# Values and gates of two HGRN2 units projected together at 512 columns, with the units of a block in another order

## The chip, the cores and the metric

The kernel runs on one core of one Trainium2 chip. The metric is device time in microseconds (us); the figure for a kernel is the median of its runs. One further execution is recorded by the hardware profiler; its time and its span (first to last instruction) stand beside the median below. The engines are named as in the profile: PE is TensorE's matmul, PEld its weight load, DVE VectorE, ACT ScalarE, POOL GpSimd, SP the engine that issues nearly all DMAs here.

## What is computed

One layer of a decoder trunk over 2048 tokens of width 1024, in float32, conditioned on a vector `c`. Cut to what matters here:

```
mod = silu(c) @ w_ada + b_ada                  # 6 x 1024
sh1, sc1, g1, sh2, sc2, g2 = split(mod, 6)
h = rms_norm(x) * (1 + sc1) + sh1
proj = h @ w_in                                # split into the three groups of heads
#   retention (4 heads), HGRN2 (8 heads: q, f, value i, gate g), GLA (4 heads)
o_h = rms_norm(gated_state(silu(q), key(f), i, log_f)) * silu(g)      # HGRN2; the others alike
x = x + g1 * (concat(o_r, o_h, o_a) * head_gain) @ w_out
h = rms_norm(x) * (1 + sc2) + sh2
u = causal_conv3(h @ w_up) + conv_b
x = x + g2 * (silu(u_gate) * u_val) @ w_down
out = rms_norm(x) * final_gain
```

The gated state is a causal recurrence with a decay for each key channel, made in chunks.

## The kernel before

**Tiling.** The sequence is cut into four blocks (`b` = 0 to 3) of 512 tokens. A matmul product of float32 precision is made of three matmuls (`split3`, L230): each operand is held as a high part (rounded to the matmul's type) and a low part (the rest), and high x high, high x low and low x high are summed in PSUM. Weights come in pieces of 128 x 1024 numbers (512 KB). `piece` (L212) loads a raw piece, ACT rounds it to the high part, and the low part is made by DVE the first time and kept in DRAM (`kept`), from which later blocks load it. There are three buffers for high parts, three for low parts and two for raw pieces.

**Units.** Seven units work on each block, in the order of `ORDER` (L35): four HGRN2 units `h` of two heads (`unit_h`, L680), one GLA unit `g` of four heads in two halves (`unit_g`, L717) and two retention units `r` (`unit_r`, L761). An h unit projects `f` and `q` with the channels on partitions (`cf_gemm`, 512 tokens as columns, tiles `pshfh` and `pshqh`), and its value and gate with the tokens on partitions (`tf_gemm`, L254, 256 columns: 128 of value, 128 of gate, tile `psvgh`). In `tf_gemm` 4 token tiles x 8 slices of the contraction x 3 give 96 matmuls of 256 columns. GLA and retention use `tf512` (L272), which takes two such column groups at a time: 96 matmuls of 512 columns into four PSUM banks. The evacuation makes a copy (value), a sigmoid on ACT and a product on DVE (gate): `tok_evac` (L510) by two token tiles at a time, `tok_evac4` (L519) by one.

**Chains.** After the projections of a unit its recurrence runs as a chain (`gated`, L579; `retention`, L793): seven levels, each of four small matmuls (L603) and some DVE operations, then the state update (`u`, which needs the value tile `v`), the output, its normalisation (`post`) and, later, a transpose (L545). PE's order is written by hand: the class `Clock` counts PE time, and the steps of the chains are put between the projection matmuls at due times. Only one chain runs at a time; the next one starts when it yields `None`.

**Other engines.** DVE, ACT, POOL and SP are ordered when the program is built, by program position; `high_priority(offset)` moves instructions ahead by that much (or back, where it is negative), and an instruction takes its place when its buffers are free by the builder's reckoning. Each engine then issues in that fixed order, SP its DMAs too.

**Work between the units.** `out_half(b, 0)` (L904), the first half of the output projection, runs at the end of block b and starts the residual tiles `x1`, loaded on the tag `xy` (four buffers, each of two tiles). `out_finish(b)` (L926) makes the second half after the first unit of block b + 1, adds the residual (L919), and its `then` (L937) scales the result for the channel mixer and stores it (`h2d`). For block 0 the `x1` tiles are stored to DRAM first, and `then` is put off to the end of block 1, with reloads. The same four `xy` buffers serve the conditioning rows (`ada`, L193: a 512 KB load `wada` and one DVE reduction each; rows still to be made stand in the list `later`, and each weight piece takes one), the sums of channel-mixer weights (`weight_sums`, tiles `wsd`, `wsu`) and the sums of scaled inputs (`early_sums`, tiles `es`). The loop over blocks and units is at L1048.

Of the kernel before, what the change touches and what calls it, by code (L numbers as in the profile page):

```python
# [9 lines left out]
F32 = mybir.dt.float32  # L10
# [21 lines left out]
NSB = 2  # L32
SB = 2 * TB

ORDER = [("h", 0), ("g", 0), ("h", 1), ("h", 2), ("h", 3), ("r", 0), ("r", 1)]  # L35
KTILES = [t for kind, u in ORDER for t in {"h": [2 + u], "g": [6, 7], "r": [u]}[kind]]


# [62 lines left out]
def trunk(ctx, tc, xT, vecs, cvec, cst, rope, msk, wada, win, walow, wgla, wout, wup, wdown, out):  # L101
# [167 lines left out]
                        adv(6 * M256)  # L269
        return pss  # L270

    def tf512(name, i):  # L272

        pss = [acc_ps(f"ps{name}_{c}") for c in range(NCH)]
        for q4 in range(4):
            half, sub = q4 // 2, q4 % 2
            src = win[i + half:i + half + 3:2][:, :, sub * 512:(sub + 1) * 512].rearrange("a p n -> p a n")
            if later:
                ada(later.pop(0))
            with tc.high_priority(offset=50):  # L280
                raw = pw.tile([P, 2, 512], F32, tag="wraw", name=f"r{name}_{q4}", bufs=NRAW)
                nc.sync.dma_start(raw[:], src)
                hi = pw.tile([P, 2, 512], F32R, tag="whi", name=f"h{name}_{q4}")
                lo = pw.tile([P, 2, 512], F32R, tag="wlo", name=f"l{name}_{q4}")
                S.copy(hi[:], raw[:])
                key = f"t{i}_{q4}l"
                flat = lo[:].rearrange("p a n -> p (a n)")
                if key in kept:
                    nc.sync.dma_start(flat.bitcast(F32), kept[key][:])
                else:  # L290
                    with tc.high_priority(offset=HOT):
                        V.tensor_tensor(lo[:], raw[:], hi[:], op=ALU.subtract)
                    keep(key, flat)
            for c in range(NCH):
                cs = slice(c * P, (c + 1) * P)
                for kk in range(2):
                    k = half * 4 + sub * 2 + kk
                    sl = slice(kk * 256, (kk + 1) * 256)
                    split3(pss[c][:].rearrange("p (a n) -> p a n", a=2), (h[k][:, 0, cs], h[k][:, 1, cs]),
                           (hi[:, :, sl], lo[:, :, sl]), k == 0, k == KD - 1)  # L300
                    adv(3 * M512)
        return pss
# [201 lines left out]

    def tok_tiles(name):

        return (pu.tile([P, NCH, P], F32, tag="v", name="v" + name, bufs=3),
                pu.tile([P, NCH, P], F32, tag="sg", name="sg" + name, bufs=3))

    def tok_evac(vsg, pss):  # L510
        v, sg = vsg
# [67 lines left out]
    def gated(name, b, ui, pos, kq, decay, subs, qk, sel):  # L579
# [56 lines left out]
                S.copy(q[r0:r1, 0, :], q[r0:r1, 1, :])  # L636
        adv(4 * MF)
        yield 1.8
        for q, rows, v, sg in subs:
            ps = late_ps("u" + name)  # L640
            for c in range(NCH):
                T.matmul(ps[:, c * P:(c + 1) * P], kT[:, c, :], v[:, c, :], start=True, stop=True)
            with tc.high_priority(offset=CHAIN):
                for c in range(NCH):
                    for hh, (r0, r1) in enumerate(rows):
                        es = slice(64 * hh, 64 * hh + 64)
                        dst = Sst[r0:r1, (b * NCH + c + 1) % NS, es]
                        u = ps[r0:r1, c * P + hh * 64:c * P + hh * 64 + 64]
                        if b == 0 and c == 0:
                            V.tensor_copy(dst, u)  # L650
                        elif c < NCH - 1 or b < NB - 1:
                            V.scalar_tensor_tensor(dst, Sst[r0:r1, (b * NCH + c) % NS, es], cur[r0:r1, c:c + 1], u,
                                                   op0=ALU.mult, op1=ALU.add)
# [23 lines left out]
            adv(4 * MF)  # L677


    def unit_h(b, u, pos):  # L680
        nm = f"h{b}_{u}"
        kq = pu.tile([P, TB], F32, tag="k", name="k" + nm, bufs=3)
        f = pu.tile([P, TB], F32, tag="f", name="f" + nm, bufs=3)
        e = pu.tile([P, TB], F32, tag="e", name="e" + nm)
        ps = cf_gemm("hf" + nm, 4 * u + 1)
        sf, sn = tmp("sf" + nm), tmp("sn" + nm)
        S.activation(sf[:], ps[:], AF.Sigmoid)
        S.activation(sn[:], ps[:], AF.Sigmoid, scale=-1.0)
        V.tensor_scalar(f[:], sf[:], oml[:, u:u + 1], lb[:, u:u + 1], op0=ALU.mult, op1=ALU.add)
        V.tensor_scalar(kq[:], sn[:], oml[:, u:u + 1], None, op0=ALU.mult)  # L690
        ps = cf_gemm("hq" + nm, 4 * u)
        sq = tmp("sq" + nm)
        S.activation(sq[:], ps[:], AF.Sigmoid)
        V.tensor_tensor(sq[:], ps[:], sq[:], op=ALU.mult)
        qk = tmp("qk" + nm)
        V.tensor_tensor(qk[:], sq[:], kq[:], op=ALU.mult)
        rows = [(0, 64), (64, 128)]
        q = new_qbd(nm, rows)
        for hh, (r0, r1) in enumerate(rows):
            V.tensor_tensor(q[r0:r1, hh, :], sq[r0:r1, :], f[r0:r1, :], op=ALU.mult)  # L700
        decay = decays(f, e)
        subs = [(q, rows, *tok_tiles(nm))]
        clock.chain(gated(nm, b, u, pos, kq, decay, subs, qk, selh), 9.0 if b == u == 0 else 6.0)
        tok_evac(subs[0][2:], tf_gemm("vg" + nm, 4 * u + 2))

    alow = p1.tile([P, KD, 32], F32R, tag="alow", name="alow")
    gup = p1.tile([32, P], F32, tag="gup", name="gup")
# [9 lines left out]
    def unit_g(b, pos):  # L717
# [37 lines left out]
        pss = tf512(f"vg{nm}", 18)  # L755
        for i in range(2):
            tok_evac4(subs[i][2:], pss, 256 * i)

    rots = {}

    def unit_r(b, r, pos):  # L761
# [2 lines left out]
            rots[b] = pu.tile([P, NCH, 2, 32], F32, tag="rope", name="rope" + nm, bufs=1)  # L764
            nc.sync.dma_start(rots[b][:], rope[b])
        cos, sin = (rots[b][:, :, i, :] for i in range(2))
        kk = pu.tile([P, NCH, P], F32, tag="kk", name="kk" + nm)
        kc = pu.tile([P, TB], F32, tag="k", name="kc" + nm, bufs=3)
        q = new_qbd(nm, [(0, 64), (64, 128)])
        vsg = tok_tiles(nm)  # L770
# [155 lines left out]
    def out_finish(b, after_pieces=None, begun=None):  # L926
# [8 lines left out]
            nc.sync.dma_start(x1d[b, m][:], rows[m])  # L935

        def then():  # L937
            with tc.high_priority(offset=HOT if b < NB - 1 else -100):
                for m in range(KD):
                    t = rows[m] if b == NB - 1 else tmp(f"t2_{b}_{m}")[:]  # L940
                    if b == 0:
                        nc.sync.dma_start(t, x1d[b, m][:])
                    else:
                        nc.sync.dma_start(x1d[b, m][:], rows[m])
                    V.scalar_tensor_tensor(t, rows[m] if b else t, SC2[:, m:m + 1], bc[:], op0=ALU.mult, op1=ALU.mult)
                    S.activation(t, t, AF.Identity, bias=SH2[:, m:m + 1])
                    nc.sync.dma_start(h2d[b, m][:], t)
            done.add(("n2", b))
# [98 lines left out]
    jobs = [job for k in range(NF // 2) for job in (("d", k), ("u", 2 * k + 1))] + [("u", 0)]  # L1047
    for b in range(NB):  # L1048
        pos = 0
        if b == NB - 1:  # L1050
            later += range(40, 48)
        for i, (kind, u) in enumerate(ORDER):
            if i == len(ORDER) - 3 and b + 1 < NB:
                norm1_stat(b + 1)
# [10 lines left out]
            pos += 2 if kind == "g" else 1  # L1065
            if b == 1 and i == 5:
                assert not later
                clock.until(lambda: put_off)
                put_off.pop()()
            if i == 0 and b:  # L1070
                clock.until(lambda: None not in oTs[b - 1])
                out_finish(b - 1)
            for w in ws:
# [484 lines left out]
```

## Time and profile before

| | |
|---|---|
| median of 3 runs | 2565.36 us (2562.51 to 2572.84) |
| profiled execution | 2567.58 us, span 2565.8 us |
| ACT, POOL busy | 1134.1 us, 160.0 us |
| DMA | 525.13 MB, mean 205 GB/s |
| mixing stage | about the first 1250 us |
| channel mixer | the rest |

In the rows, L232 to L234 are the three matmuls of `split3`, whatever product they belong to, so products are told apart by the tile that they write. A group's line gives busy time and mean duration; durations of matmuls overlap, so starts, not durations, give the rate. In a timeline row stand start, duration, engine, line, operation, output and inputs, and in brackets the idle time before it and what ended that.

### The profile page before, as it was taken

How to read it: one execution, taken by the hardware profiler on the slowest of the kernel's cores; microseconds unless marked ns; L12 is line 12 of the kernel's file. 1: busy time of each engine (PE TensorE's matmuls, PEld its weight loads, DVE VectorE, ACT ScalarE, POOL GpSimd, SP SyncE). 2: the span in 40 equal slices, each digit the busy share in tenths (PEclk: the TensorE clock that was granted, in tenths of full speed). 3: DMA queues.
4: the chain of work that ended last, by engine and by line, in shares of the span. 5: the costliest groups of instructions: out<-in, count | busy, mean ns of one | idle time of the engine just before them, and what ended most of it. 6: DMA issues, size and time to landing. Idle time of an engine off the chain costs nothing.

```text
span 2565.8 us, 36953 instructions
## 1 busy us (share of the span) xinstructions
PE 2485.1 (97%) x13090; PEld 2122.6 (83%) x13090; DVE 1996.1 (78%) x3626; ACT 1134.1 (44%) x1890; POOL 160.0 (6%) x287
## 2 busy tenths in 40 slices
PE   5999999999999998999999999999999999999998
PEld 4898888988889896898778888888878888888887
DVE  8877888767679777686788888887688778778666
ACT  3333334434443334333554545555444554455542
POOL 1000010000000000000010000000001001000000
PEclk9999999999999999999999999999999999999999
DMA  8644468654598747985654445477675454447763
GB/s 307 219 165 132 150 221 312 231 181 160 195 317 295 272 157 233 320 309 186 202 187 162 153 149 163 157 239 257 219 225 186 150 154 145 146 142 245 225 190 132
DMA packets 227721, 525.13 MB, mean 205 GB/s; under 512 B 25264, under 2 KB 28368, under 8 KB 227536
## 3 DMA queue, kind: packets, MB, share of 16 engines
q1 hardware_dynamic: 224336, 512.28, 60.2%
q0 software_dynamic: 3200, 10.49, 1.2%
q8 instruction: 103, 1.69, 0.3%
q14 instruction: 82, 0.67, 0.1%
HBM read 397.37 MB, written 125.30 MB: 204 GB/s over the span
## 4 chain that ended last, share of the span: by engine, by line
PE 87%; DVE 6%; DMA 2%; issue 1%; ACT 1%; POOL 0%; SPq 0%; DVEq 0%; ACTq 0%; POOLq 0%
PE X L232 6%; PE X L234 6%; PE X L233 6%; PE lvh L603 4%; PE Z L233 3%; PE Z L234 3%; PE dX L234 3%; PE Z L232 3%; PE dX L233 3%; PE dX L232 3%; PE psqkvgr L234 2%; PE psqkvgr L232 2%; PE psqkvgr L233 2%; PE lvg L603 2%; PE psvgh L232 2%; PE psvgh L234 2%
## 5 line engine op out<-in xcount | busy, mean ns | idle before, releaser
L232 PE MATMUL X<-B,A 128*128 128x512 f32 x572 | 223.6, 391 | 1.4 <-ACT u L1265 1.4
L233 PE MATMUL X<-B,A 128*128 128x512 f32 x572 | 222.8, 390 | 0.0
L234 PE MATMUL X<-B,A 128*128 128x512 f32 x572 | 222.8, 390 | 0.0
L980 DVE TENSOR_TENSOR dA<-rd,dA 128x512 fp32r<-128x512 f32 x154 | 106.0, 689 | 83.5 <-ACT dA L979 83.3
L979 ACT CAST dA<-rd 128x512 fp32r<-128x512 f32 x154 | 95.6, 621 | 134.1 <-PE dY L234 40.5
L980 DVE TENSOR_TENSOR A<-s,A 128x512 fp32r<-128x512 f32 x176 | 120.6, 686 | 41.0 <-ACT A L979 40.8
L232 PE MATMUL psvgh<-hvgh,ha 128*128 128x256 f32 x480 | 139.8, 291 | 0.0
L979 ACT CAST A<-s 128x512 fp32r<-128x512 f32 x176 | 108.7, 618 | 65.3 <-PE Z L234 45.2
L232 PE MATMUL dX<-dB,dA 128*128 128x512 f32 x352 | 136.9, 389 | 0.0
L233 PE MATMUL dX<-dB,dA 128*128 128x512 f32 x352 | 136.9, 389 | 0.0
L234 PE MATMUL dX<-dB,dA 128*128 128x512 f32 x352 | 136.9, 389 | 0.0
L234 PE MATMUL psvgh<-hvgh,ha 128*128 128x256 f32 x480 | 135.7, 283 | 0.0
L233 PE MATMUL psvgh<-lvgh,ha 128*128 128x256 f32 x480 | 135.6, 283 | 0.0
L232 PEld LDWEIGHTS X<-B,A 128*128 128x128 f32 x572 | 107.7, 188 | 24.4 <-ACT u L1265 2.3
L234 PEld LDWEIGHTS X<-B,A 128*128 128x128 f32 x572 | 107.5, 188 | 22.5
L233 PEld LDWEIGHTS X<-B,A 128*128 128x128 f32 x572 | 107.7, 188 | 22.3
L603 PEld LDWEIGHTS lvh<-qbh,kh 128*128 128x128 f32 x896 | 115.9, 192 | 10.6 <-issue 3.5
L603 PE MATMUL lvh<-qbh,kh 128*128 128x128 f32 x896 | 121.0, 278 | 2.8 <-DVE kh L613 1.5
L233 PE MATMUL Z<-B,A 128*128 128x512 f32 x308 | 120.1, 390 | 2.6 <-DVE B L980 2.6
L232 PE MATMUL Z<-B,A 128*128 128x512 f32 x308 | 119.9, 389 | 0.0
L234 PE MATMUL Z<-B,A 128*128 128x512 f32 x308 | 119.8, 389 | 0.0
L980 DVE TENSOR_TENSOR dB<-rb,dB 128x512 fp32r<-128x512 f32 x154 | 105.4, 686 | 12.6 <-ACT dB L979 12.5
(456 smaller groups left out, 7111.1 us busy)
## 6 DMA issues: line engine op xcount, KB each, us to landing
gs<-yv SPq DMA_DIRECT2D x154, 256.0 KB, 3.0
rb<-gs SPq DMA_DIRECT2D x154, 256.0 KB, 4.2
r<-wup SPq DMA_DIRECT2D x140, 256.0 KB, 3.5
s<-sumsu SPq DMA_DIRECT2D x136, 256.0 KB, 3.2
wada<-wada SPq DMA_DIRECT2D x48, 512.0 KB, 6.1
rd<-sumsd SPq DMA_DIRECT2D x88, 256.0 KB, 4.2
rd<-wdown SPq DMA_DIRECT2D x66, 256.0 KB, 4.0
x<-xT SPq DMA_DIRECT2D x64, 256.0 KB, 5.7
```

The lines of the kernel that those rows point to most:

```text
L232: T.matmul(ps, lhs[0], rhs[0], start=first, stop=False, skip_group_check=more)
L233: T.matmul(ps, lhs[0], rhs[1], start=False, stop=False, skip_group_check=more)
L234: T.matmul(ps, lhs[1], rhs[0], start=False, stop=last, skip_group_check=more)
L603: T.matmul(ps[:, c * P:(c + 1) * P].rearrange("p (h n s) -> p h n s", h=2, s=s), kq[:, c * P:(c + 1) * P], rhs, start=True, stop=True)
L979: S.copy(hi, src)
L980: V.tensor_tensor(lo, src, hi, op=ALU.subtract)
```

## The change

1. `ORDER` becomes h0, h1, g, h2, h3, r0, r1 (it was h0, g, h1, ...). The rows of `w_out` and the gains follow through `KTILES`, on the host.
2. Value and gate of the units (0, 1) and (2, 3) are projected together by `tf512` with a step of 4 between the weight pieces, 512 columns, after `f` and `q` of the second of the two. In block 0 the units 0 and 1 keep `tf_gemm`. Low parts kept by single pieces are loaded in two halves. Both units are evacuated by `tok_evac4`.
3. A chain waits, in steps of 1.0 us of the clock, ahead of its state update until its value tile is made (`tokens`).
4. `v` and `sg` get four buffers in place of three; the retention tile `kk` uses the tag `e` in place of its own.
5. `out_finish(b - 1)` runs after the second unit of a block, not the first.
6. The put-off `then` of block 0 has priority -100, not `HOT` (600).
7. Conditioning rows 40 to 47 (`G2`) are asked for from the sixth unit of block 1 on, not from the start of block 3. The conditions that start rows 16 to 23 (third unit of block 0) and 24 to 39 (second unit of block 1) stay as they are, in the new order.

```diff
--- before.py
+++ after.py
@@ -32,7 +32,7 @@
 NSB = 2
 SB = 2 * TB
 
-ORDER = [("h", 0), ("g", 0), ("h", 1), ("h", 2), ("h", 3), ("r", 0), ("r", 1)]
+ORDER = [("h", 0), ("h", 1), ("g", 0), ("h", 2), ("h", 3), ("r", 0), ("r", 1)]
 KTILES = [t for kind, u in ORDER for t in {"h": [2 + u], "g": [6, 7], "r": [u]}[kind]]
 
 
@@ -269,12 +269,12 @@
                         adv(6 * M256)
         return pss
 
-    def tf512(name, i):
+    def tf512(name, i, step=2):
 
         pss = [acc_ps(f"ps{name}_{c}") for c in range(NCH)]
         for q4 in range(4):
             half, sub = q4 // 2, q4 % 2
-            src = win[i + half:i + half + 3:2][:, :, sub * 512:(sub + 1) * 512].rearrange("a p n -> p a n")
+            src = win[i + half:i + half + step + 1:step][:, :, sub * 512:(sub + 1) * 512].rearrange("a p n -> p a n")
             if later:
                 ada(later.pop(0))
             with tc.high_priority(offset=50):
@@ -285,8 +285,12 @@
                 S.copy(hi[:], raw[:])
                 key = f"t{i}_{q4}l"
                 flat = lo[:].rearrange("p a n -> p (a n)")
+                one = [f"i{i + half + step * a}l" for a in range(2)]
                 if key in kept:
                     nc.sync.dma_start(flat.bitcast(F32), kept[key][:])
+                elif one[0] in kept:
+                    for a in range(2):
+                        nc.sync.dma_start(lo[:, a, :].bitcast(F32), kept[one[a]][:, sub * 512:(sub + 1) * 512])
                 else:
                     with tc.high_priority(offset=HOT):
                         V.tensor_tensor(lo[:], raw[:], hi[:], op=ALU.subtract)
@@ -504,8 +508,8 @@
 
     def tok_tiles(name):
 
-        return (pu.tile([P, NCH, P], F32, tag="v", name="v" + name, bufs=3),
-                pu.tile([P, NCH, P], F32, tag="sg", name="sg" + name, bufs=3))
+        return (pu.tile([P, NCH, P], F32, tag="v", name="v" + name, bufs=4),
+                pu.tile([P, NCH, P], F32, tag="sg", name="sg" + name, bufs=4))
 
     def tok_evac(vsg, pss):
         v, sg = vsg
@@ -636,6 +640,8 @@
                 S.copy(q[r0:r1, 0, :], q[r0:r1, 1, :])
         adv(4 * MF)
         yield 1.8
+        while name not in tokens:
+            yield 1.0
         for q, rows, v, sg in subs:
             ps = late_ps("u" + name)
             for c in range(NCH):
@@ -677,6 +683,8 @@
             adv(4 * MF)
 
 
+    tokens, waiting = set(), {}
+
     def unit_h(b, u, pos):
         nm = f"h{b}_{u}"
         kq = pu.tile([P, TB], F32, tag="k", name="k" + nm, bufs=3)
@@ -701,7 +709,16 @@
         decay = decays(f, e)
         subs = [(q, rows, *tok_tiles(nm))]
         clock.chain(gated(nm, b, u, pos, kq, decay, subs, qk, selh), 9.0 if b == u == 0 else 6.0)
-        tok_evac(subs[0][2:], tf_gemm("vg" + nm, 4 * u + 2))
+        if b == 0 and u < 2:
+            tok_evac(subs[0][2:], tf_gemm("vg" + nm, 4 * u + 2))
+            tokens.add(nm)
+            return
+        waiting[nm] = subs[0][2:]
+        if u % 2:
+            pss = tf512("vg" + nm, 4 * u - 2, 4)
+            for i, one in enumerate((f"h{b}_{u - 1}", nm)):
+                tok_evac4(waiting.pop(one), pss, 256 * i)
+                tokens.add(one)
 
     alow = p1.tile([P, KD, 32], F32R, tag="alow", name="alow")
     gup = p1.tile([32, P], F32, tag="gup", name="gup")
@@ -755,6 +772,7 @@
         pss = tf512(f"vg{nm}", 18)
         for i in range(2):
             tok_evac4(subs[i][2:], pss, 256 * i)
+        tokens.add(nm)
 
     rots = {}
 
@@ -764,7 +782,7 @@
             rots[b] = pu.tile([P, NCH, 2, 32], F32, tag="rope", name="rope" + nm, bufs=1)
             nc.sync.dma_start(rots[b][:], rope[b])
         cos, sin = (rots[b][:, :, i, :] for i in range(2))
-        kk = pu.tile([P, NCH, P], F32, tag="kk", name="kk" + nm)
+        kk = pu.tile([P, NCH, P], F32, tag="e", name="kk" + nm)
         kc = pu.tile([P, TB], F32, tag="k", name="kc" + nm, bufs=3)
         q = new_qbd(nm, [(0, 64), (64, 128)])
         vsg = tok_tiles(nm)
@@ -935,7 +953,7 @@
             nc.sync.dma_start(x1d[b, m][:], rows[m])
 
         def then():
-            with tc.high_priority(offset=HOT if b < NB - 1 else -100):
+            with tc.high_priority(offset=HOT if 0 < b < NB - 1 else -100):
                 for m in range(KD):
                     t = rows[m] if b == NB - 1 else tmp(f"t2_{b}_{m}")[:]
                     if b == 0:
@@ -1047,8 +1065,6 @@
     jobs = [job for k in range(NF // 2) for job in (("d", k), ("u", 2 * k + 1))] + [("u", 0)]
     for b in range(NB):
         pos = 0
-        if b == NB - 1:
-            later += range(40, 48)
         for i, (kind, u) in enumerate(ORDER):
             if i == len(ORDER) - 3 and b + 1 < NB:
                 norm1_stat(b + 1)
@@ -1065,9 +1081,10 @@
             pos += 2 if kind == "g" else 1
             if b == 1 and i == 5:
                 assert not later
+                later += range(40, 48)
                 clock.until(lambda: put_off)
                 put_off.pop()()
-            if i == 0 and b:
+            if i == 1 and b:
                 clock.until(lambda: None not in oTs[b - 1])
                 out_finish(b - 1)
             for w in ws:
```

## The prediction

> **What bounds the kernel now.** I read the page from the top: busy times, then the chain that ended last.
>
> ```profile
> span 2565.8 us, 36953 instructions
> PE 2485.1 (97%) x13090; PEld 2122.6 (83%) x13090; DVE 1996.1 (78%) x3626; ACT 1134.1 (44%) x1890; POOL 160.0 (6%) x287
> ...
> PE 87%; DVE 6%; DMA 2%; issue 1%; ACT 1%; POOL 0%; SPq 0%; DVEq 0%; ACTq 0%; POOLq 0%
> ```
>
> TensorE is busy 97% of the span and carries 87% of the chain, so only two things shorten this kernel: less matmul time, or fewer holes in it. The waits of TensorE in the mixing stage (0 to 1260 us) list the holes (total, times, longest):
>
> ```profile
> PE psvgg L233 <- DMA lvgg<-keptt_2l: 15.4, 1, 15.4
> ...
> PE oTh L545 <- DVE oh L539: 4.0, 1, 4.0
> ...
> PE pshfh L232 <- ACT ha L343: 1.6, 1, 1.6
> ```
>
> The first is one wait for a weight load in the g unit of block 3; the second is one wait near the end of block 1. Both lie where the change moves work. The third, at block 0's end, and the start-up are left alone.
>
> **Part 1, the projections.** How long a matmul occupies the array is read from starts, since the durations overlap. The timeline of TensorE, start and duration first; the outer rows of two unbroken runs:
>
> ```profile
> 128.08 0.29 PE L234 MATMUL psvgh<-hvgh,ha 128*128 128x256 f32 x1
> ...
> 132.76 0.28 PE L234 MATMUL psvgh<-hvgh,ha 128*128 128x256 f32 x1
> ...
> 230.00 0.39 PE L234 MATMUL psqkvgr<-hqkvgr,ha 128*128 128x512 f32 x1
> ...
> 232.72 0.39 PE L234 MATMUL psqkvgr<-hqkvgr,ha 128*128 128x512 f32 x1
> ```
>
> The first run has 39 steps in 4.68 us: 0.120 us for 256 columns. The second has 12 in 2.72 us: 0.227 us for 512. The groups by line give the count:
>
> ```profile
> L234 PE MATMUL psvgh<-hvgh,ha 128*128 128x256 f32 x480 | 135.7, 283 | 0.0
> ```
>
> Each of the three lines of a split product has 480, so 1440 matmuls, 96 for each of 15 units (unit 0 of block 0 is made at start-up). Unit 1 of block 0 keeps its 96; the other 14 units become 7 pairs. So 1344 x 0.120 = 161.3 us go and 672 x 0.227 = 152.5 us come: **-8.8 us**, all on the bounding engine.
>
> The Trainium skill, "TensorE: Matmul & The Clock Gate", section "Back-to-back issue gap", speaks against that size: it puts the warm gap at N/2.4 + 2.5 ns, an estimate of 109 and 216 ns here, by which the saving would be 1.7 us. The rows above differ from it (120 and 227 ns), and they decide.
>
> Weight traffic stays at four 512 KB pieces a pair. For the first pair of blocks 1 to 3 each low part comes by two DMAs, 12 more issues at 0.32 to 0.38 us on SP (rows below), some 4 us hidden in a queue that mostly waits for buffers; uncovered they would cost 4 us.
>
> The evacuation is split finer. From the views by tile (min/median/max ns):
>
> ```profile
> L515 ACT COPY vh<-psvgh x32: 353/373/416, 59.1 to 1144.7; 128x256 f32<-128x256 f32 x32
> L516 ACT ACTIVATE sgh<-psvgh x32: 379/390/452, 59.4 to 1144.9; 128x256 f32<-128x256 f32 x32
> ...
> L524 ACT COPY vg<-psvgg x32: 259/266/298, 101.5 to 1049.1; 128x128 f32<-128x128 f32 x32
> L525 ACT ACTIVATE sgg<-psvgg x32: 277/284/333, 103.1 to 1049.3; 128x128 f32<-128x128 f32 x32
> ```
>
> A pair had 4 of each of the first two and gets 8 of each of the last two: 4.4 us of ACT instead of 3.1, hidden by an engine that is busy 44%; DVE's products are cut in half likewise. The g unit already evacuates four banks this way, and no wait for its banks stands among the holes, so I take 0; uncovered it is 1.3 us a pair, 9 in all. The new wait is that a chain's `u` comes only after its pair's projection. Behind it on TensorE stands the rest of the program, and it waits for the last copy: between 0 and copy plus sigmoid (0.55 us) with some latency, 0 to 1 us for each of 7 pairs. I take +2.
>
> **Part 2, the hole in block 3.** SP's timeline (its DMA issues; the duration includes blocking) from the last weight load before the hole to the one TensorE waited for, and TensorE after it:
>
> ```profile
> 996.29 0.32 SPq L289 DMA_DIRECT2D lvgg<-keptt_1l  x1
> 997.78 3.33 SPq L947 DMA_DIRECT2D h2d<-t  x5
> 1001.50 0.76 SPq L190 DMA_DIRECT2D wada<-wada  x1
> 1002.37 3.09 SPq L947 DMA_DIRECT2D h2d<-t  x3
> 1005.55 10.31 SPq L190 DMA_DIRECT2D wada<-wada  x7
> 1017.54 1.53 SPq L872 DMA_DIRECT2D wsd<-wdown  x2
> 1020.92 2.00 SPq L1012 DMA_DIRECT2D es<-h2d  x4
> 1023.02 0.38 SPq L289 DMA_DIRECT2D lvgg<-keptt_2l  x1
> ...
> 1029.98 0.80 PE L233 MATMUL psvgg<-lvgg,ha 128*128 128x512 f32 x1 [15.37 <-DMA lvgg<-keptt_2l]
> ...
> 1033.06 0.39 PE L234 MATMUL psvgg<-hvgg,ha 128*128 128x512 f32 x1
> ```
>
> SP issues in the order of the program. The eight conditioning rows (`wada`) share the four `xy` buffers with the residual tiles of block 2, so they queue until `out_finish` lets those go, and the weight load stands behind them. After the hole 7 matmuls take 3.08 us instead of 7 x 0.227 = 1.59: a slow clock adds 1.5. Price of the hole: 15.4 + 1.5 = 16.9 us.
>
> The change makes these rows in block 1. Without them the load is issued earlier by 1017.54 - 1005.55 + 0.87 = 12.9 us, at 1010.1; it took 7.0 us to land (1023.02 to 1029.98), so 1017.1, and TensorE wanted it at 1029.98 - 15.37 = 1014.6: a rest of 2.5 us. A landing in 4.5 us leaves none. But h1's chain now runs beside the start of g, and the eight `h2d` stores wait for DVE, which serves that chain. I keep +4 of 16.9: **-12.9 us**; the bounds are -16.9 and 0. What is late next there are the weight sums and early sums, which stand between the stores and the load.
>
> Block 2 has the same order without the rows:
>
> ```profile
> 695.28 0.32 SPq L289 DMA_DIRECT2D lvgg<-keptt_1l  x1
> ...
> 705.19 0.38 SPq L289 DMA_DIRECT2D lvgg<-keptt_2l  x1
> ```
>
> 9.9 us apart, and no hole. In block 3 it was 26.7 us with a hole of 15.4, so the hole opens at 11.3 us. Block 2 has little to spare: +1 for its denser start.
>
> In block 1 rows 24 to 39 are asked for from h1 on, ten of them before g begins, and wait for `out_finish(0)` to free `xy`. Before, they were asked for from g on, and five went through SP in one stretch ahead of a weight load:
>
> ```profile
> 376.84 11.84 SPq L190 DMA_DIRECT2D wada<-wada  x5
> 388.77 0.38 SPq L289 DMA_DIRECT2D lvgg<-keptt_1l  x1
> ```
>
> No hole followed, so I take 0; uncovered, the price is that of block 3's hole. Rows 40 to 47 come later, beside r1 and the first half of the output projection, ahead of that projection's residual loads on `xy`. The last of those loads and their first use in block 1, then the same in block 2 (its first loads):
>
> ```profile
> 477.69 0.42 SPq L913 DMA_DIRECT2D x<-xT  x1
> ...
> 592.29 0.74 DVE L919 SCALAR_TENSOR_TENSOR x<-y,mod,x 128x512 f32<-128x512 f32 x1
> ...
> 860.24 3.85 SPq L913 DMA_DIRECT2D x<-xT  x5
> ...
> 893.45 0.75 DVE L919 SCALAR_TENSOR_TENSOR x<-y,mod,x 128x512 f32<-128x512 f32 x1
> ```
>
> In block 1 eight rows at 2.4 us (11.84/5), 19 us, hide in 114. In block 2 cover is thinner: its `xy` work starts later by 10.9 + 21.8 - 11.5 = 21.2 us of matmuls (48 x 0.227, 96 x 0.227, 96 x 0.120), with the chain's between them some 27 (my choice). 860.2 + 27 = 887.2 leaves 6.3 us to land, where a load above took 7.0. Between 0 and 3 us; I take +1.
>
> **Part 3, the wait of 4.0 us.** DVE and then TensorE near the end of block 1:
>
> ```profile
> 572.25 0.75 DVE L945 SCALAR_TENSOR_TENSOR t<-t,mod,bc 128x512 f32<-128x512 f32 x1 [0.62 <-DMA t<-x1d]
> ...
> 573.85 0.68 DVE L539 TENSOR_TENSOR oh<-oh,sgh 128x512 f32<-128x512 f32 x1
> ...
> 574.68 0.63 PE L545 MATMUL oTh<-c_all,oh 128*128 128x128 f32 x4 [3.96 <-DVE oh L539]
> ...
> 575.62 0.63 PE L234 MATMUL psqkvgr<-hqkvgr,ha 128*128 128x512 f32 x1
> ...
> 579.02 0.40 PE L232 MATMUL psqkvgr<-hqkvgr,ha 128*128 128x512 f32 x1
> ```
>
> The put-off scaling of block 0 (L945) runs at the highest priority, waits for its reloads on the in-order DVE and pushes the head's normalisation back. From 575.62 to 579.02 a matmul shows 0.63 us instead of 0.39, about half speed, so half of 3.4 us goes too: 4.0 + 1.7 = 5.7 us. At priority -100 those eight come after the chain's work. I take **-4.7**, keeping 1 for reloads that still block DVE; bounds -5.7 and 0.
>
> How much a short new wait costs is read from block 0's end, in the windows (the column after POOL's is the clock):
>
> ```profile
> 312.00:316.00 4.00, 3.49 (x16) 3.30 (x16) 2.38 (x4) 0.72 (x1) 0.00 (x0) 0.59 0.00 0
> ```
>
> This follows the wait of 1.6 us, and loses 0.4 x 4 = 1.6 us more: a short wait costs about double. The Trainium skill's same page, section "What's actually happening", asks for an idle window of about 3.4 us before the clock halves; here less was enough. By the page the +2 above would stay +2, by the row it may be +4.
>
> The rest (`e` shared with `kk`, four `v` and `sg` buffers for three) costs 0: r0's `kk` needs h2's chain to be past its states, and h3's chain stands between them. If that cover goes, DVE waits for the rest of a chain, some 4 us.
>
> **Sum.** The profiled execution took 2567.6 us (span 2565.8 and 1.8 around it), 2.2 above the median of the runs. -8.8 + 2 - 12.9 + 1 + 1 - 4.7 = -22.4: 2545.2 on its own scale, **2543** on the median's.
>
> **Rivals.** *All holes close, block 0's too* (1.6 + 1.6), at full prices: -8.8 - 16.9 - 5.7 - 3.2 = -34.6, 2531; chance 0.07. For: order changes there too; against: nothing aims at it.
>
> *The hole stays, with other goods in it.* Two groups of weight sums and early sums now stand behind `out_finish(2)`. If the second is issued ahead of the weight load, SP blocks about as long as before, and only the rest of the sum counts: -8.8 + 4 - 4.7 = -9.5, 2556; 0.19. Against: the second group's buffers come free only when the first's sums are stored.
>
> *Slower.* The place is SP between the second and third weight load of g; the mechanism is `h2d` stores held back by a DVE that also serves h1's chain (blocks 2 and 3), and in block 1 sixteen rows in a row. It decides where that gap passes 11.3 us. Three holes of 16.9 in place of one: -8.8 - 5.7 + 2 x 16.9 = +19.3, 2585; 0.09. For: DVE is at 78%; against: block 2's gap is 9.9 us.
>
> *512 columns buy nothing*, since 256 would take half of 0.227 in the long run: 2543 + 8.8 = 2552; 0.05, against 39 even steps. The gap formula cited above would nearly give this.
>
> **How the numbers follow.** My forecast, 2533 to 2552, has the remaining 0.60. About 0.5% (13 us) is what a measurement of this kernel can tell from no change. Faster by more (below 2552.5): 0.60 + 0.07 + 0.05 = 0.72; within: 0.19; slower: 0.09. The range takes in the forecast, the 512 case, the edge of the first rival and most of the staying hole: 2531 to 2560.
>
> **What would show it.** Right: 672 more 512-column matmuls 0.227 us apart; no wait of `psvgg` for `keptt_2l` above 4 us; no wait of `oTh` of 4 us in block 1; no `wada` in block 3. Wrong: a new wait for a weight load in g or the pairs, `u` waiting for `v`, or L919 waiting for `x<-xT`.

## The result, and the profile after

The changed kernel takes **2594.38 us** (median of 4 runs, 2592.75 to 2597.17), the kernel before in the same session 2568.95 us (4 runs, 2562.51 to 2572.84): a ratio of 1.0103, with a 95% interval of 1.0076 to 1.0129. The change makes the kernel 1% slower; the prediction was 2543 us, range 2531 to 2560.

The page of the changed kernel, first the span and the busy times, then the chain that ended last:

```profile
span 2592.4 us, 35722 instructions
PE 2495.8 (96%) x12418; PEld 2098.8 (81%) x12418; DVE 1993.2 (77%) x3654; ACT 1138.3 (44%) x1946; POOL 160.3 (6%) x287
...
PE 76%; DVE 12%; DMA 6%; issue 3%; ACT 1%; SPq 0%; DVEq 0%; ACTq 0%; POOL 0%; POOLq 0%
```

There are 672 matmuls fewer (13090 before), as intended, yet TensorE is busy 10.7 us longer. Its part of the chain fell from 87% to 76%; DVE's rose from 6% to 12% and DMA's from 2% to 6%. So the time went into waits, and into a slower clock behind them (0.987 in the mean, 0.992 before). The waits of TensorE from 0 to 1300 us (total, times, longest) say for what; the start-up's rows are left out:

```profile
PE psvgg L232 <- ACT hvgg L285: 9.9, 2, 6.0
PE pshqh L234 <- DMA lhqh<-kepti12l: 6.4, 1, 6.4
PE oTh L549 <- DVE oh L543: 5.7, 4, 4.6
PE bcn L326 <- DVE S L658: 5.3, 2, 2.6
...
PE psvgh L232 <- DVE sqh L702: 3.7, 1, 3.7
...
PE psvgh L232 <- ACT hvgh L285: 3.3, 2, 1.7
```

The wait of 15.4 us for `keptt_2l` is gone and so is the one of 4.0 us at 574 us. In their place stand a dozen waits of 1 to 6.4 us: for weight pieces of g and of h3, for the broadcast of the statistics (`bcn`), for the head's normalisation in another place of block 1, and for q. The wait of `bcn` is not for the statistics alone: in block 1 `rsn` was made by 507.7 us and `bcn` started at 511.8, while DVE made g's state update `S`, whose input `ug` uses the same two PSUM buffers (tag `late`).

How far each block is hit, I read from the first start of its `f` matmuls to the first `psqkvgr` (the stretch of the h and g units; block 0 from 58.2 us), in us. e4, e6, e9, e10, e11, e15 and e18 are experiments told below.

| block | before | after | e4 | e6 | e9 | e10 | e11 | e15 | e18 |
|---|---|---|---|---|---|---|---|---|---|
| 0 | 150.8 | 153.3 | 150.3 | 159.6 | 147.8 | 148.5 | 142.9 | 143.5 | 143.0 |
| 1 | 217.8 | 224.8 | 217.0 | 230.3 | 216.0 | 212.2 | 219.8 | 219.4 | 219.2 |
| 2 | 203.5 | 220.4 | 203.5 | 214.7 | 200.5 | 201.6 | 208.0 | 198.7 | 198.7 |
| 3 | 218.0 | 208.6 | 204.2 | 202.7 | 202.6 | 204.3 | 206.9 | 208.5 | 199.7 |

From e9 on the statistics of the next block are begun with r0, outside this stretch. That alone shortens it: e10 differs from e4 by this only, and is some 8 us below e4 in the table and 2.8 us above it in time. So what the later statistics are worth is read from the times.

Block 3 gained 9.4 us, of 12.9 that the prediction promised it. Block 2, which it had at +1, lost 16.9. There lie the two longest new waits, 6.4 and 6.0 us. For the second, SP's timeline in block 2, start and duration first, then TensorE's:

```profile
744.73 0.32 SPq L965 DMA_DIRECT2D h2d<-t  x1
...
746.62 0.38 SPq L290 DMA_DIRECT2D lvgg<-keptt_2l  x1
752.11 2.00 SPq L902 DMA_DIRECT2D sumsd<-wsd  x2
755.19 2.35 SPq L902 DMA_DIRECT2D sumsu<-wsu  x2
757.60 1.26 SPq L890 DMA_DIRECT2D wsd<-wdown  x2
758.90 2.11 SPq L890 DMA_DIRECT2D wsu<-wup  x2
761.05 0.66 SPq L282 DMA_DIRECT2D rvgg<-win  x1
```

```profile
764.00 0.39 PE L234 MATMUL psvgg<-hvgg,ha 128*128 128x512 f32 x1
770.42 0.79 PE L232 MATMUL psvgg<-hvgg,ha 128*128 128x512 f32 x1 [6.03 <-ACT hvgg L285]
771.01 0.63 PE L233 MATMUL psvgg<-lvgg,ha 128*128 128x512 f32 x1
```

The raw fourth piece of g (`rvgg`) is issued 14.4 us after the low third; in the kernel before it was 0.4 us (705.19 and 705.62). In between SP issues the stores of one group of weight sums, most of whose waiting is for DVE to make them, and then the loads of the next group into the same buffers. ACT cannot round a piece that has not come, so TensorE waits 6.03 us "for ACT", and the matmuls behind take 0.63 us each in place of 0.39.

### The profile page after: what moved, and what is told of

Same layout as the page of the kernel before. It is cut to its first block, busy times and chain, and to the rows that moved or that the text cites. A ratio compares the mean times of both kernels' runs of the same rounds, so it can differ in the third digit from the quotient of the medians.

```text
span 2592.4 us, 35722 instructions
## 1 busy us (share of the span) xinstructions
PE 2495.8 (96%) x12418; PEld 2098.8 (81%) x12418; DVE 1993.2 (77%) x3654; ACT 1138.3 (44%) x1946; POOL 160.3 (6%) x287
## 4 chain that ended last, share of the span: by engine, by line
PE 76%; DVE 12%; DMA 6%; issue 3%; ACT 1%; SPq 0%; DVEq 0%; ACTq 0%; POOL 0%; POOLq 0%
PE X L232 6%; PE X L234 6%; PE X L233 6%; PE Z L233 3%; PE Z L234 3%; PE lvh L607 3%; PE Z L232 3%; PE dX L233 3%; PE dX L232 3%; PE dX L234 3%; PE psvgh L232 2%; PE psvgh L233 2%; PE psvgh L234 2%; PE psqkvgr L232 2%; PE psqkvgr L234 2%
## 5 line engine op out<-in xcount | busy, mean ns | idle before, releaser
L998 DVE TENSOR_TENSOR A<-r,A 128x512 fp32r<-128x512 f32 x130 | 89.3, 687 | 28.5 <-ACT A L997 28.5
L232 PE MATMUL psvgh<-hvgh,ha 128*128 128x512 f32 (+1 forms) x256 | 103.1, 403 | 7.0 <-DVE sqh L702 3.7
L232 PE MATMUL psqkvgr<-hqkvgr,ha 128*128 128x512 f32 x256 | 106.2, 415 | 2.4 <-DVE sgh L530 1.7
```

Of the source, the lines that this page charges most:

```text
L232: T.matmul(ps, lhs[0], rhs[0], start=first, stop=False, skip_group_check=more)
L998: V.tensor_tensor(lo, src, hi, op=ALU.subtract)
```

## The experiments

Each is timed in three rounds beside the kernel before, whose median was 2566.8 to 2569.9 us in the five sessions; ratios are to it. Medians of different sessions are compared as they stand, which can be some 3 us off. Three theories stood at the start. **Queue**: `out_finish`, one unit later, holds the `xy` buffers longer, so weight sums stand ahead of weight loads in SP's order. **Order**: g's long chain now runs beside h2 and h3 and crowds DVE. **Bank**: a pair wants four PSUM banks right behind q, whose bank DVE gives back late.

### e1 and e2: one part of the change undone

e1 undoes the late `out_finish`, e2 the pairs:

```diff
-            if i == 1 and b:          # e1
+            if i == 0 and b:
-        if b == 0 and u < 2:          # e2
+        if True:
```

> The changed kernel, but out_finish(b - 1) runs after the first unit of a block again. Queue theory (the later out_finish holds the xy buffers longer, so that weight sums stand ahead of weight loads in SP's queue): the waits for weights in blocks 2 and 3 (6.0, 6.4 and 3.9 us) and some 10 us of slow clock after them go, 2568 us. Order theory (what costs is that g's chain now runs beside the next block's statistics on DVE): these waits are a by-product, the 2.6 us waits of bc for S in blocks 1 and 2 stay, at most 5 us gained, 2590 us.

> The changed kernel in its new order, with 256 columns for all units (no pair). Bank theory (a pair takes four PSUM banks right after q and frees them by sixteen small operations, so it waits for DVE): the waits at the pairs' start and end (3.7, 1.6, 1.5, 1.7, 0.8 us and some 7 us of slow clock) go, the saved matmul time of 5 to 9 us is lost, 2583 to 2587 us. If the pairs are innocent, only the matmul time is lost: 2600 to 2603 us.

e1: 2595.34 us, 1.0109 (1.0094 to 1.0124); e2: 2585.54 us, 1.0067 (1.0047 to 1.0086). TensorE's waits in e1, 58 to 1240 us:

```profile
PE psvgh L232 <- DVE sqh L702: 15.5, 3, 6.1
PE bcn L326 <- DVE S L658: 7.0, 2, 4.4
```

No wait for a weight piece is left among e1's large ones, so the queue theory is right about their cause; but waits for DVE of the same size stand in their place and nothing is won. e2 lies where the bank theory had it (2583 to 2587). It shows that the pairs, which should save 8.8 us, cost 8.9 here. Even so, the kernel without pairs is far above the one before.

### e3 and e4: the two confirmed steps alone

e3 is the kernel before with rows 40 to 47 in block 1; e4 has the low priority of the put-off `then` as well.

```diff
-        if b == NB - 1:
-            later += range(40, 48)
...
                 assert not later
+                later += range(40, 48)
...
-            with tc.high_priority(offset=HOT if b < NB - 1 else -100):      # e4
+            with tc.high_priority(offset=HOT if 0 < b < NB - 1 else -100):
```

> The kernel before with one edit: conditioning rows 40 to 47 asked for in block 1. My step 2: the 15.4 us hole of block 3 and its 1.5 us of slow clock go and nothing else opens, 2549 us, at worst a rest of 4 us, 2553. Rival: the hole is filled by other loads and stays, 2566.

> As the run with the rows moved alone, and the put-off scaling of block 0 at priority -100 too. My step 3: the 4.0 us wait of oTh at the end of block 1 and 1.7 us of slow clock go as well, 2544 us. Rival: the scaling is late elsewhere and gives nothing, 2549 us.

e3: 2555.52 us, 0.9956 (0.9939 to 0.9973), 12.1 below the kernel before. e4: 2548.80 us, 0.9926 (0.991 to 0.9942), another 6.7. Each missed its expected figure by 5 to 7 us, though part 2 and part 3 alone are worth what the prediction gave them. In e3 the wait at 574 us is still there, in e4 its rest is small (waits of TensorE, first e3, then e4):

```profile
PE oTh L545 <- DVE oh L539: 4.1, 1, 4.1
```

```profile
PE oTh L545 <- DVE oh L539: 1.1, 1, 1.1
```

So pairs, order and late `out_finish` together cost 45.6 us over e4, and e4 is the fastest kernel of this study.

### e5 to e8: order, pair and q apart

e5 is the changed kernel without pairs and with the early `out_finish`, hence e4 in the new order, with the buffers and the chain's wait of the change (points 3 and 4). e6 is e4 with one pair a block, units 2 and 3, in the old order. e7 is e1, and e8 is e6, with the evacuation of q moved ahead.

```diff
-        S.activation(sq[:], ps[:], AF.Sigmoid)                       # e7, e8
-        V.tensor_tensor(sq[:], ps[:], sq[:], op=ALU.mult)
+        with tc.high_priority(offset=HOT):
+            S.activation(sq[:], ps[:], AF.Sigmoid)
+            V.tensor_tensor(sq[:], ps[:], sq[:], op=ALU.mult)
-ORDER = [("h", 0), ("h", 1), ("g", 0), ("h", 2), ...                 # e6, e8
+ORDER = [("h", 0), ("g", 0), ("h", 1), ("h", 2), ...
-        if b == 0 and u < 2:
+        if u < 2:
```

> The changed kernel with every projection at 256 columns (no pairs) and the second half of the output projection after the first unit again: it differs from the kernel before plus moved rows plus low priority (2548.8 us) almost only by the order h0, h1, g. Queue theory (the late second half of the output projection holds the shared buffers, so weight-sum stores stand ahead of weight loads in SP's queue): with it early again the holes of 6.0, 6.4 and 5.2 us before psvgg and pshqh go, 2553 to 2560 us. Order theory (g's long chain beside the projections of h2 and h3 and the next block's statistics costs in itself): most of the 37 us stays, 2572 to 2582 us.

> The order of before (h0, g, h1, h2, h3), second half of the output projection early, the pair only for the units 2 and 3 of every block. By starts a pair is worth 1.26 us, four of them 5.0 us: 2544 us if nothing stops them (from 2548.8). Bank theory (the pair wants four banks at once right behind q, whose bank DVE gives back late): each of four pairs waits 4 to 6 us and is followed by a slow clock, 2560 to 2575 us.

> The changed kernel with the early second half of the output projection (2595.3 us) and the evacuation of q (sigmoid and product) moved ahead on ACT and DVE by 600 places. Bank theory: the three waits of 3.7, 6.1 and 5.7 us of psvgh for DVE's product of q go, with about as much of slow clock behind them: 2568 to 2576 us. If those waits only stand in for others (order theory alone), 2588 to 2596 us.

> The order of before, one pair (units 2 and 3) in each block, and the evacuation of q moved ahead as in the run before this one. 2540 to 2546 us where the bank is all that can stop a pair; 2548 to 2556 us where moving q ahead takes DVE from the chain, whose small matmuls then wait.

e5: 2616.65 us, 1.0185 (1.0168 to 1.0202). e6: 2586.21 us, 1.0073 (1.0053 to 1.0093). e7: 2591.85 us, 1.0092 (1.0071 to 1.0113). e8: 2586.30 us, 1.0072 (1.0052 to 1.0092). e5, e6 and e8 lie above all that was expected of them; e7 lies where the order theory alone had it.

The bank theory falls: with q ahead, e7 is 3.5 us under e1 and e8 is equal to e6. In e7 (its profile is of the slowest of its runs) two of the three waits for q are still there:

```profile
PE psvgh L232 <- DVE sqh L703: 11.5, 2, 5.9
```

The instruction may stand first in DVE's order, but DVE is late as a whole.

e6 is the surprise: four pairs, with the buffers and the finer evacuation that belong to them, cost 37.4 us over e4. The table of blocks shows where: +9.3, +13.3 and +11.2 in blocks 0 to 2, and -1.5 in block 3, close to the 1.26 us that a pair is worth (8.8 / 7). What blocks 0 to 2 have and block 3 has not are the statistics of the next block's first norm (`norm1_stat`, begun with h3). The windows of e4, then e6, in block 1 (busy us of PE, PEld, DVE, ACT, POOL, then the clock):

```profile
486.00:494.00 8.00, 8.00 (x49) 6.91 (x48) 8.00 (x16) 4.66 (x8) 0.00 (x0) 1.00 0.78 276
494.00:502.00 8.00, 8.00 (x49) 7.00 (x48) 7.21 (x15) 4.93 (x8) 0.00 (x0) 1.00 0.64 215
```

```profile
486.00:494.00 8.00, 8.00 (x42) 6.79 (x42) 7.74 (x16) 4.35 (x8) 0.17 (x1) 1.00 0.88 292
494.00:502.00 8.00, 2.90 (x17) 2.19 (x15) 7.83 (x25) 3.10 (x5) 0.00 (x0) 0.83 0.95 352
502.00:510.00 8.00, 3.76 (x15) 3.60 (x16) 7.90 (x24) 0.69 (x1) 0.00 (x0) 0.50 0.63 197
```

DVE is full in both. In e4 the work just fits; in e6 TensorE stands behind a transpose whose input `og` DVE has not made. The waits of e6 (380 to 545 us) name `nw`, the small operation right behind it; DVE's timeline has `og`, and the transpose starts at 506.24 us:

```profile
PE oTg L549 <- DVE nw L156: 9.3, 1, 9.3
```

```profile
505.40 0.69 DVE L543 TENSOR_TENSOR og<-og,sgg 128x512 f32<-128x512 f32 x1
```

This gives a new theory, **crowding**: the value and gate projection of h2, 11.5 us of matmuls with little for DVE, lay between q of h2 and f of h3. The pair takes it away, and h3's f and q and the statistics reach DVE while it is still at the chains before.

### e9 to e12: the statistics one unit later

The same edit in e6 (e9), in e4 (e10, the control), in the changed kernel (e11) and in e1 (e12):

```diff
-            if i == len(ORDER) - 3 and b + 1 < NB:
+            if i == len(ORDER) - 2 and b + 1 < NB:
                 norm1_stat(b + 1)
```

> The order of before with one pair a block (2586.2 us), where the statistics of the next block's first norm are begun one unit later (with r0, not with h3). The pair takes away the value and gate projection of h2, the stretch in which DVE used to catch up, so f and q of h3 and the statistics come 10 us earlier onto a DVE that is still at g's and h1's chains; the blocks 0, 1 and 2, which have statistics, lost 9.3, 13.3 and 11.2 us, block 3, which has none, gained 1.5. Crowding theory: without the statistics there the pair is worth its matmuls again, 2542 to 2550 us. Bank theory: 2578 to 2588 us.

> The control: the kernel before with moved rows and low priority (2548.8 us) and the statistics one unit later. No pair, so nothing to be freed: 2546 to 2551 us by both theories. Under 2543 us, the place of the statistics would be worth something by itself.

> The changed kernel (2594.4 us) with the statistics one unit later. Crowding theory: the waits for the statistics (bcn, 2.6 us in block 1 and in block 2, 1.5 us after it) go with their slow clock, the waits for weight loads in blocks 2 and 3 stay: 2578 to 2587 us. If the long chain of g beside h2 and h3 is crowded enough by itself: 2590 to 2597 us.

> The changed kernel with the second half of the output projection early (2595.3 us) and the statistics one unit later: waits for weight loads and for statistics both gone. 2575 to 2585 us if the two causes add; 2590 to 2597 us if the early second half crowds the pair (0, 1) as the statistics crowd the pair (2, 3).

e9: 2552.99 us, 0.994 (0.9924 to 0.9956). e10: 2551.58 us, 0.9936 (0.9915 to 0.9958). e11: 2577.93 us, 1.0036 (1.0024 to 1.0048). e12: 2576.75 us, 1.0033 (1.002 to 1.0046).

In the old order, the crowding theory is shown: the edit takes 33.2 us off e6 and nothing off e4. In the 24 us from 486 us on, DVE is busy 98% in e6 and 70% in e9, TensorE 61% and 98%. The middle window of e9:

```profile
494.00:502.00 8.00, 8.00 (x43) 6.79 (x42) 6.08 (x11) 3.23 (x5) 0.00 (x0) 1.00 0.86 294
```

What is left of the waits of e9 from 380 to 545 us:

```profile
PE psqkvgr L232 <- DVE nw L157: 1.7, 1, 1.7
PE lvh L607 <- DVE kh L617: 0.5, 1, 0.5
```

But e9 lies 3 us above the range that the theory gave it and is no faster than e10: the four pairs are not seen in the time even here.

The changed kernel gains 16.5 us by the edit, as that theory had it, and stays 26 us above e10. But not all of this is crowding on DVE: the wait of 6.4 us for h3's `lhqh` in block 2, a weight load that was expected to stay, goes too, as it did in e1 (e11's waits from 760 to 840 us do not have it). In the changed kernel that load stood on SP behind the statistics' own loads (L481) and a store of sums:

```profile
792.96 1.67 SPq L220 DMA_DIRECT2D rhqh<-win  x1
...
797.15 3.14 SPq L481 DMA_DIRECT2D x<-xT  x5
803.51 0.33 SPq L902 DMA_DIRECT2D sumsu<-wsu  x1
...
804.41 0.74 SPq L223 DMA_DIRECT2D lhqh<-kepti12l  x1
```

How the 16.5 divide between DVE and SP no run shows. e12 lies where the two causes were to add, but it is no faster than e11: two waits for q, 10.1 us in all, are still there. Why the early `out_finish` brings them was not settled.

### e13, e14, e16: what the order costs

e13 and e14 are e2 and e5 with the statistics late. e16 is e12 with g ahead of all h units in blocks 1 to 3:

```diff
-        for i, (kind, u) in enumerate(ORDER):                        # e16
+        for i, (kind, u) in enumerate(ORDER if b == 0 else ORDER[2:3] + ORDER[:2] + ORDER[3:]):
```

> The new order without pairs, second half of the output projection late, statistics late. If the pairs hold the rest of the loss: near the old order without pairs, 2551 to 2558 us. If the order (with what it does to SP's queue) holds it: 2578 to 2587 us, since the pairs then save their 7 us of matmuls in the kernel with pairs (2577.9 us).

> As the run before this one, with the second half of the output projection early. It was 2616.7 us with the statistics beside h3, of which its waits for statistics (2.4, 5.5 and 4.3 us, with a slow clock) go: 2590 to 2600 us if the order is what costs, since chains then run late to the end of each block; 2552 to 2560 us if crowding by the statistics was all of it.

> From the changed kernel with early second half and late statistics (2576.8 us): in blocks 1 to 3 g is the first unit, then h0, h1, h2, h3 with both pairs. Crowding theory: g's long chain runs beside h0 and h1, where no statistics run, and the pair (2, 3) finds DVE free, but the second half of the output projection and its scaling now stand right behind g: 2555 to 2570 us. If two projections of f and q in a row are what crowds DVE wherever they stand: 2575 to 2590 us.

e13: 2583.93 us, 1.0068 (1.0053 to 1.0083). e14: 2596.52 us, 1.0116 (1.0099 to 1.0133). e16: 2575.81 us, 1.0035 (1.0024 to 1.0047).

Medians in us, by order, `out_finish` and pairs:

| | statistics with h3 | with r0 |
|---|---|---|
| old order, early, no pairs | 2548.8 (e4) | 2551.6 (e10) |
| old order, early, one pair a block | 2586.2 (e6) | 2553.0 (e9) |
| new order, late, no pairs | 2585.5 (e2) | 2583.9 (e13) |
| new order, late, pairs | 2594.4 (changed) | 2577.9 (e11) |
| new order, early, no pairs | 2616.7 (e5) | 2596.5 (e14) |
| new order, early, pairs | 2595.3 (e1) | 2576.8 (e12) |

With late statistics the pairs of the changed kernel save 6.0 us (e13 to e11; 8.2 by the ratios, as the sessions differ), while the new order costs 32 us without any pair (e10 to e13). So most of what the statistics leave belongs to the order, with the late `out_finish` that goes with it; the buffers and the chain's wait are in e9 too, which is only 1.4 us above e10. With the early one the pairs seem to save 20 us, more than their matmuls can. Without them TensorE waits where they have no such wait (e5, 58 to 1240 us):

```profile
PE or L563 <- DVE oTh L553: 15.2, 2, 7.6
...
PE dth L596 <- ACT t L964: 8.0, 2, 4.1
```

These four stand at the ends of blocks 1 and 2, and in h1 of the next block, which waits for the scaling behind `out_finish`. Why just this combination makes them was not settled. Nor does g first help: in e16 the largest wait is now for g's own state (58 to 1240 us), and the time stays that of e12. It lies where it was expected if two projections of `f` and `q` in a row crowd DVE wherever they stand, which no run tests by itself.

```profile
PE og L563 <- DVE S L658: 10.9, 3, 4.8
```

### e15, e17, e18: the weight sums moved away from g's loads

From e11. e15 begins the weight sums of block 2 with the third unit; e17 those of block 3 too; e18 also begins the early sums one unit later. The groups left over go to later units of blocks 1 and 3.

```diff
-            if b and i >= (3 if b == 1 else 1):
+            if b and i >= (3 if b == 1 else 2 if b == 2 else 1):     # e15
+            if b and i >= (3 if b == 1 else 2):                      # e17, e18
-            if b == NB - 1 and 1 <= i <= 4:                          # e18
-                es = early_sums_load(i - 1)
+            if b == NB - 1 and 2 <= i <= 5:
+                es = early_sums_load(i - 2)
```

> The changed kernel with late statistics (2577.9 us), where block 2 begins its weight sums with the third unit, not with the second; one group goes to the end of block 1, one to the end of block 3, so block 3 still has sums beside its second unit and is the control. Queue theory: in block 2 the wait of 4.8 us for g's last weight piece goes, and 1 to 2 us of slow clock with it, in block 3 it stays at 4: 2571 to 2574 us. If the sums do not hold that piece up: 2577 to 2580 us with the wait at its place.

> As the run with the weight sums of block 2 moved (2561.5 us), with those of block 3 begun with the third unit too. The early sums stay beside the second unit. Queue theory: g's last weight piece in block 3 now waits behind the early sums alone, its wait falls from 3.5 us to under 1, the clock stays full there: 2554 to 2558 us. If the early sums alone hold it: 2560 to 2563 us.

> As the run before this one, with the early sums also one unit later (a further group of weight sums goes to block 1 for them). Queue theory: no wait for a weight piece of g is left in blocks 2 and 3: 2551 to 2556 us. It would stay above the old order without pairs (2548.8 us) by what is left: 4.6 us at oTh in block 1.

e15: 2561.45 us, 0.9975 (0.9966 to 0.9985). e17: 2560.30 us, 0.9976 (0.9963 to 0.9989). e18: 2560.73 us, 0.9979 (0.9967 to 0.9991).

The waits of TensorE in block 2 (690 to 930 us), first e11, then e15:

```profile
PE psvgg L232 <- ACT hvgg L285: 4.8, 1, 4.8
PE psvgh L232 <- ACT hvgh L285: 1.7, 1, 1.7
```

```profile
PE pshfh L232 <- DVE sgg L530: 1.0, 1, 1.0
```

And SP of e15 at the place that held g's fourth piece:

```profile
735.30 0.88 SPq L890 DMA_DIRECT2D wsd<-wdown  x2
736.27 0.38 SPq L290 DMA_DIRECT2D lvgg<-keptt_2l  x1
736.71 0.46 SPq L282 DMA_DIRECT2D rvgg<-win  x1
```

The raw piece follows 0.4 us behind the low one, not 14.5 as in e11, and the waits are gone; block 2 falls by 9.3 us, block 3, the control, does not (208.5 against 206.9). The queue theory is shown for block 2. The size is less sure: e15 was expected at 2571 to 2574 us. The medians differ by 16.5, the spans of the profiled executions by 7.8; e11's runs spread from 2569.95 to 2582.59 us, and its profile is of the fastest.

In block 3 the same move takes g's wait for its weight piece away and 4.0 us off the stretch (e17: 204.5), and the early sums give 4.8 us more (e18: 199.7). But the medians do not follow: e17 lies where the early sums alone were to hold the piece up, e18 some 5 us above its range. In e17 a wait of 3.2 us that e15 does not have stands behind block 3 (a matmul of `X` for ACT at 1277.6 us). In e18, which sends one more group to block 1 than e17, the time from that block's first `psqkvgr` to the `f` of block 2 is 113.4 us, against 105.7 in e17, with the second wait below in it (waits of e18, 58 to 1240 us). That the extra group causes it fits, but no run shows it.

```profile
PE oTh L549 <- DVE oh L543: 5.3, 4, 4.6
PE y L232 <- DVE sgr L530: 3.6, 1, 3.6
```

## Why the prediction was wrong, step by step

**Part 1, -8.8 for the matmuls: the mechanism right, the size about three quarters.** In place, from start to start and without the waits, the 1344 matmuls of 256 columns took 165.0 us before, 123 ns each; the 672 of 512 columns 158.1 us in e11, 235 ns each, so 6.9 us less, and e13 to e11 gives 6.0 by the medians, 8.2 by the ratios. The prediction took rates of unbroken runs, 120 and 227 ns; in the stage the chains break them. In the changed kernel the pairs took 163.9 us with its slow clock, and the gain was 1.1. The gap formula of the Trainium skill, "TensorE: Matmul & The Clock Gate", section "Back-to-back issue gap", from which the prediction's estimate was 1.7, lies further from the 6.9 than the trace's rate did. That section of the Trainium skill gives the formula for a matmul by itself and says that it is off in a stream of weight loads and matmuls, for which it has about 131 ns at 512 columns; here the measured steps of 227 to 235 ns decide.

**"The evacuation is split finer ... I take 0": the step that failed, with its cover.** It counted what the pair adds to DVE and ACT and asked whether that is hidden. It did not ask what the removed projection had been hiding. That was the statistics, which cost 9 to 13 us a block in e6 and, begun later, nothing that is seen (e9); h3's f and q came early too, but their share was not tested apart. In the changed kernel the statistics at that place cost 16.5 us (e11), through DVE and through SP's queue. Nothing in the prediction's sum had a term for them, since the change doesn't move them: their neighbours moved.

**"Block 2 ... +1 for its denser start": failed.** It cost 16.9 us in the units of block 2, of which the late statistics gave back 12.4 (e11; some 2 of it only leave the stretch, as e4 and e10 show) and moving the weight sums another 9.3 (e15), together more than was lost. This is the larger miss: the new order with its late `out_finish` costs 32 us without any pair (e10 to e13), and this +1 was all that the sum had for it. The prediction had seen both causes. It named the weight sums as what is late next in block 3, and made "If the second is issued ahead of the weight load" the condition of a rival. But it priced the rival for block 3 alone, as a hole that stays, when block 2 has two groups a unit where block 3 has one. The place of the slower rival was right within one load, its mechanism was not: the gap that it went by was 11.2 us (`keptt_1l` at 735.43 to `keptt_2l` at 746.62), the `h2d` stores were through at 745 us, before the low third was issued, and behind it the sums' own stores held SP. It gave 2585 for three holes of 16.9; what came was a dozen shorter ones.

**Part 2, -12.9 for the hole of block 3: right.** e3 measures -12.1. In the changed kernel a wait of 3.9 us stays in block 3, about the 4 that were kept, but for g's fourth piece, not its third, so that this size fits is luck.

**Part 3, -4.7: right, a little small.** e3 to e4 measures -6.7 by the medians, past the bound of -5.7, and -4.3 by the spans of the profiled executions (2553.0 and 2548.7), where the wait itself falls by 3.0; the intervals are some 8 us wide. In the changed kernel a like wait (4.6 us) comes back under the late `out_finish` at 399 us, which nothing had priced.

**The new wait of `u` for `v`, +2:** none is seen among the waits of the changed kernel; the one wait of `u` there, 1.7 us in block 1, is for the copy of `kT`. The residual loads of blocks 1 and 2 (L919, +1) made none either.

**"A short wait costs about double": too high for these.** After the wait of 6.03 us the clock is half for 5 us (window from 770 us, last section), a loss of 2.5. Behind two waits of 2.6 us the loss is 1.7 and nothing.

**The account.** From e4, which holds the steps that were right, to the changed kernel it is +45.6 us: 16.5 for the place of the statistics beside the pair, then by the medians 16.5 for the weight sums of block 2 (7.8 by the two profiles), and some 13 that is left between e15 and e4, after what the pairs save. Of those, the trace of e15 names waits of 3.5 and 1.7 us for weight pieces in block 3 and of 4.6 us in block 1; the rest of the price of the order stays open.

## What to carry to other kernels

Before two stages are merged, ask what work on the other engines the removed stage was covering, and who stands next to it afterwards: DVE, busy 78% in the mean of the kernel before, was busy 98% for the 24 us in which e6 lost most. A DMA queue that issues in order, as SP's here, has to be read as a list after every change of order, block by block, since a store or load that waits delays every load behind it (14.4 us in block 2 here). And undoing parts one at a time is not enough where causes stand in for one another: e1 took a cause away and won nothing, because the next one was as long.

## What the runs showed of the hardware

The clock after a short wait is not a function of the wait's length alone. Two waits of the changed kernel are alike to 10 ns, behind the same matmuls (`ug`); TensorE's timeline, and the windows behind each:

```profile
511.78 0.62 PE L326 MATMUL bcn<-c_all,rsn 128*128 128x128 f32 x4 [2.64 <-DVE S L658]
...
838.19 0.62 PE L326 MATMUL bcn<-c_all,rsn 128*128 128x128 f32 x4 [2.63 <-DVE S L658]
```

```profile
512.00:516.00 4.00, 4.00 (x14) 3.18 (x13) 3.87 (x10) 1.63 (x2) 0.00 (x0) 0.57 0.62 231
...
770.00:775.00 5.00, 4.58 (x11) 3.62 (x12) 0.84 (x2) 3.01 (x5) 0.00 (x0) 0.50 0.89 260
...
838.20:842.00 3.80, 3.80 (x22) 3.28 (x23) 2.93 (x12) 1.64 (x2) 0.00 (x0) 1.00 0.58 194
```

The first wait is followed by a clock of 0.57 and 14 matmuls in 4 us, the second by full speed. The Trainium skill, "TensorE: Matmul & The Clock Gate", section "What's actually happening", speaks of an idle window of about 3.4 us; the second wait is in line with it, the first is not, and what tells the two apart these runs do not show.
